# v and z_a of two pairs of heads in one product, with three of eight k-tile pairs as seven products

## The chip, the cores and the metric

The kernel runs on one core of one Trainium2 chip. The metric is the device time of one execution in microseconds. The kernel before takes 1117.3 us (median of 3 runs, 1116.82 to 1117.96). TensorE is PE in the profile, its weight loads PEld, VectorE DVE, ScalarE ACT, GpSimd POOL and SyncE SP.

## The reference

One encoder layer on 256 tokens of width 2048 in f32. Cut to what matters:

```python
hn = rmsnorm(x, norm_w)
q, v, f_fwd, f_bwd, z_a, b_gate, c_gate, h_b, z_b = split(hn @ w_in)      # nine times 2048 columns
o_a = hgrn2(silu(q), v, f_fwd, lb[0]) + hgrn2(silu(q), v, f_bwd, lb[1], reversed)
o_a = head_rmsnorm(o_a, hgrn_norm_w) * silu(z_a)                          # 16 heads of 128
y_b = b_gate * conv3(c_gate * h_b)
o_b = rmsnorm(y_b, conv_norm_w) * silu(z_b)
h = x + concat(o_a, o_b) @ w_out
h = h + (p @ w_ple) * sigmoid(h @ w_ple_gate)
out = rmsnorm(h, final_norm_w)
```

The recurrence runs in chunks of 64 tokens: with the cumulated logarithms of the forget gates f, q and k = 1 - f are scaled, their products are masked (scores), and the scores and the carried states are multiplied with v (outputs).

## The kernel before, in words

*Precision.* Every f32 operand is kept as a high part (rounded to fp32r) and a low part (the rest). One product of 128 rows of k is three matmuls: high x high, high x low, low x high. So every weight passes through `Stream.split` (L98 to L100): ACT casts it to the high part, DVE subtracts. `Stream` loads 1 MB pieces (`raw`, three buffers) on SP's queue, splits them into parts (`spl`, five buffers) and is asked for three parts ahead (`get`).

*Stages.* The layer's 16 heads are eight pairs; `two_pairs(i)` does pairs i and i+1 for i = 0, 2, 4, 6. For each pair it computes f_fwd, f_bwd and q in column-major form, heads on the partitions (`gemm_in`, L378 and L376, 16 k-tiles of four matmuls each), and `evac` (L410, L411) takes the two accumulators out: ACT copies the second half to `r`, DVE adds the first half. Then v and z_a of both pairs, 512 columns each, in token-major form: `gemm_two` (L397 to L399), first v with all 16 k-tiles, then z_a. The accumulators are four banks of PSUM (tag `g`), taken in turn, two by each of these products. After the four groups come the 32 column-major products of branch B, then the output projection `w_out` and the gate `w_ple_gate`.

*Seven products.* The output projection already does four of each eight pairs of k-tiles as seven products of sums instead of eight products (Strassen's scheme, `half`, `three`). The sums of weights are made in DRAM: `prepare` copies the blocks on SP's queue, and `add_up` adds onto them with accumulating DMAs that POOL issues, in three steps, each of which reads what the step before has written. `pump` issues one step; it is called at three places of each pair's attention and once per block of B.

*Attention.* Of a pair: `mix_forgets` (L455) scales f and q by the norms on POOL (`by_norms`, L415), then ACT's sigmoid of f (L459), logarithms `lf` (L469) and the sigmoid of q (L461). `mix_pair` (L513) does scans, exponentials and products, and ends on POOL with `kc`, `qc` (L557) and `kx` (L563). `scores` are 80 small matmuls into banks `sc0`, `sc1` and `x`; `outputs` go to bank `y`; `turn` (L499) transposes a finished pair with PE into `mixa` (L507, L508).

*Order.* The text is recorded with a count of ticks (one per k-tile of `gemm_in`, two per k-tile of v or z_a): `at(n, f)` records f n ticks later, in the middle of the matmuls. A scheduler then sets the order on each engine by priorities: splits and evacuations have high priority, DMAs of `prepare` and `add_up` keep their place in the program's order. Each engine takes its own queue in order.

## Time and profile before

| what | value |
| --- | --- |
| time, median of 3 runs | 1117.3 us (1116.82 to 1117.96) |
| the profiled execution | 1116.78 us, span 1115.1 us |
| PE busy | 1105.2 us (99%) |
| DVE busy | 795.0 us (71%) |
| ACT busy | 660.4 us (59%) |
| POOL busy | 258.8 us (23%) |
| v and z_a of group 2 | 192.3 to 245.1 us of the span, DVE 40.0 us, ACT 35.6 us |
| v and z_a of group 4 | 311.7 to 364.5 us |
| v and z_a of group 6 | 431.1 to 483.9 us |
| DMA | 260.43 MB, mean 234 GB/s |

Times in a timeline are microseconds from the span's start. A row gives start, duration, engine, line, operation and out<-in; a bracket gives the idle time of the engine before it and what ended that. In a row of stretches the engines stand in the order PE, PEld, DVE, ACT, POOL, each with busy time and count, then the granted TensorE clock, the DMA engines' busy share and GB/s. DMA-issuing instructions of POOL have rows of their own.

### The profile page before, as it was taken

Reading aid. Unit: us, or ns where it says so; the run is one execution under the profiler, and the core shown is the slowest. Engines: PE = TensorE matmul, PEld = TensorE weight load, DVE = VectorE, ACT = ScalarE, POOL = GpSimd, SP = SyncE. Lnnn points to the kernel's source line nnn. Section 1 sums busy time; section 2 is a strip of 40 time slices with the busy share of each in tenths; the row PEclk is TensorE's granted clock in tenths of the full one; section 3 lists DMA queues with packets and bytes.
Section 4 is the critical chain, followed back from the end, with each engine's and each line's share of the span. In section 5 each row is a group of like instructions: output and inputs, shape, how many; then the busy total and the mean of one; then the engine's idle time right before and its main releaser. Section 6 shows DMA issues by size and latency. Waiting matters only on the chain.

```text
span 1115.1 us, 16704 instructions
## 1 busy us (share of the span) xinstructions
PE 1105.2 (99%) x6482; PEld 950.5 (85%) x6482; DVE 795.0 (71%) x1040; ACT 660.4 (59%) x920; POOL 258.8 (23%) x215
## 2 busy tenths in 40 slices
PE   9999999999999999999999999999999999999996
PEld 8888888888888888888888888888888888888886
DVE  7898466955967586855666767766657878887663
ACT  7796566756865586664454544544546565575553
POOL 1144026410533036422232231322221000000101
PEclk9999999999999999999999999999999999999999
DMA  9746848765688557859897898887867887887542
GB/s 346 279 171 229 280 171 226 190 208 189 201 261 275 184 173 198 228 184 287 282 230 220 246 279 287 223 225 221 236 184 278 320 295 282 290 311 254 190 132 76
DMA packets 58287, 260.43 MB, mean 234 GB/s; under 512 B 6240, under 2 KB 6624, under 8 KB 40672
## 3 DMA queue, kind: packets, MB, share of 16 engines
q1 hardware_dynamic: 48960, 242.24, 62.7%
q0 software_dynamic: 8960, 16.78, 11.0%
q8 instruction: 51, 0.84, 0.3%
q10 hardware_dynamic: 288, 0.34, 0.1%
q14 instruction: 28, 0.23, 0.1%
HBM read 257.25 MB, written 35.65 MB: 263 GB/s over the span
## 4 chain that ended last, share of the span: by engine, by line
PE 99%; ACT 0%; DVE 0%; DVEq 0%; issue 0%; ACTq 0%
PE a L378 37%; PE a L376 19%; PE a L399 5%; PE a L397 5%; PE a L398 5%; PE pg L844 3%; PE pg L845 3%; PE pg L843 3%; PE pa L850 2%; PE pa L851 2%; PE pa L852 2%; PE pb_sc L852 1%; PE pb_sc L851 1%; PE pb_sc L850 1%; PE scps L577 1%; PE cx L621 1%
## 5 line engine op out<-in xcount | busy, mean ns | idle before, releaser
L100 DVE TENSOR_TENSOR spl<-raw,spl 128x1024 fp32r<-128x1024 f32 (+2 forms) x401 | 491.8, 1237 | 225.4 <-ACT spl L99 223.5
L378 PE MATMUL a<-xs,spl 128*128 128x512 f32 x1792 | 620.0, 394 | 0.0
L99 ACT CAST spl<-raw 128x1024 fp32r<-128x1024 f32 (+2 forms) x401 | 400.6, 1006 | 262.5 <-PE a L376 157.8
L376 PE MATMUL a<-xs,spl 128*128 128x256 f32 x1792 | 493.9, 278 | 0.0
L378 PEld LDWEIGHTS a<-xs,spl 128*128 128x128 f32 x1792 | 335.2, 188 | 76.3
L376 PEld LDWEIGHTS a<-xs,spl 128*128 128x128 f32 x1792 | 336.2, 188 | 2.1 <-DVE spl L100 0.2
L397 PE MATMUL a<-spl,xs 128*128 128x512 f32 x256 | 100.8, 394 | 0.0
L399 PE MATMUL a<-spl,xs 128*128 128x512 f32 x256 | 99.8, 390 | 0.0
L398 PE MATMUL a<-spl,xs 128*128 128x512 f32 x256 | 99.7, 389 | 0.0
L410 ACT COPY r<-a 128x256 f32<-128x256 f32 x112 | 40.8, 367 | 50.3 <-PE a L376 50.3
L1008 POOL TENSOR_TENSOR hh<-hh,fw 128x512 f32<-128x512 f32 (+1 forms) x9 | 11.0, 1226 | 251.4 <-ACT gt L1007 248.8
L399 PEld LDWEIGHTS a<-spl,xs 128*128 128x128 f32 x256 | 48.1, 188 | 10.1
L397 PEld LDWEIGHTS a<-spl,xs 128*128 128x128 f32 x256 | 48.1, 188 | 9.5
L398 PEld LDWEIGHTS a<-spl,xs 128*128 128x128 f32 x256 | 48.1, 188 | 9.5
L415 POOL TENSOR_TENSOR xf<-xf,rbc 128x1024 f32<-128x1024 f32 x8 | 21.1, 2640 | 129.0 <-DVE xf L411 122.1
L843 PE MATMUL pg<-spl,ht 128*128 128x512 f32 (+1 forms) x120 | 45.2, 377 | 0.0
L844 PE MATMUL pg<-spl,ht 128*128 128x512 f32 (+1 forms) x120 | 45.1, 376 | 0.0
L845 PE MATMUL pg<-spl,ht 128*128 128x512 f32 (+1 forms) x120 | 45.1, 376 | 0.0
L557 POOL TENSOR_TENSOR qc<-pf,ge 128x256 f32<-128x256 f32 x16 | 33.8, 2118 | 36.1 <-ACT ge L544 18.2
L99 ACT CAST spl<-early 128x1024 fp32r<-128x1024 f32 (+1 forms) x29 | 28.7, 990 | 19.8 <-PE pb_y L852 7.5
L100 DVE TENSOR_TENSOR spl<-early,spl 128x1024 fp32r<-128x1024 f32 (+1 forms) x29 | 33.0, 1148 | 10.0 <-ACT spl L99 9.5
L850 PE MATMUL pa<-spl,mixa 128*128 128x512 f32 x88 | 34.5, 392 | 0.0
(275 smaller groups left out, 1389.4 us busy)
## 6 DMA issues: line engine op xcount, KB each, us to landing
raw<-in_w_in_dram SPq DMA_DIRECT2D x106, 1024.0 KB, 6.4
raw<-in_w_in_dram SPq DMA_DIRECT2D x74, 512.0 KB, 5.1
raw<-in_w_out_dram SPq DMA_DIRECT2D x36, 512.0 KB, 5.2
sums<-in_w_out_dram SPq DMA_DIRECT2D x32, 512.0 KB, 8.3
raw<-sums SPq DMA_DIRECT2D x13, 1024.0 KB, 6.0
raw<-in_w_gate_dram SPq DMA_DIRECT2D x9, 1024.0 KB, 5.0
sums<-in_w_out_dram POOLq DMA_DIRECT2D x16, 512.0 KB, 8.1
sums<-sums POOLq DMA_DIRECT2D x32, 256.0 KB, 5.6
```

The lines of the kernel that those rows point to most:

```text
L99: self.nc.scalar.copy(out=v[:, :, 0], in_=r)
L100: self.nc.vector.tensor_tensor(out=v[:, :, 1], in0=r, in1=v[:, :, 0], op=ALU.subtract)
L376: pe.matmul(a[:, :T], lhsT=lhsT, rhs=xs[:, kt, 0, :], start=False, stop=(kt == NKT - 1))
L378: pe.matmul(a, lhsT=lhsT, rhs=xs[:, kt, :, :].rearrange("p s n -> p (s n)"), start=(kt == 0), stop=False)
L397: pe.matmul(acc[m], lhsT=lh, rhs=w[:, kt % 2, 0, :], start=(kt == 0), stop=False)
L398: pe.matmul(acc[m], lhsT=lh, rhs=w[:, kt % 2, 1, :], start=False, stop=False)
L399: pe.matmul(acc[m], lhsT=ll, rhs=w[:, kt % 2, 0, :], start=False, stop=(kt == NKT - 1))
L410: act.copy(out=r, in_=acc[m][:, 1, :])
L843: pe.matmul(acc[m], lhsT=lh, rhs=wh, start=(kt == 0), stop=False)
L844: pe.matmul(acc[m], lhsT=lh, rhs=wl, start=False, stop=False)
L845: pe.matmul(acc[m], lhsT=ll, rhs=wh, start=False, stop=(kt == nk - 1))
L850: pe.matmul(acc, lhsT=ah, rhs=w[:, 0], start=start, stop=False)
```

## The change

In groups 2, 4 and 6 `gemm_vz` takes the place of two `gemm_two`: v and z_a are one product with 1024 columns over eight pairs of k-tiles, in four accumulators (all four banks). Pairs 2, 4 and 6 of the k-tiles are seven products, with the extra four accumulators in `x`, `y`, `sc0` and `sc1`. In the first and the last pair v's part of both k-tiles comes ahead of z_a's. Group 0 is as before. The sums of x are made once, in group 2 (`xsums`); the sums of the weights of each group in DRAM, by nine steps at ticks 24 to 96 of the group, with four of w_out's steps set among them. `pump` is no longer called in the attention, but twice per block of B. Since `x`, `y`, `sc0` and `sc1` are in use, of the attention only the first pair's scores stay in v and z_a; the second pair's scores, both outputs and the turns go to the column-major products behind (or, for group 6, to B's first ones). The values are scaled by the norms after the combination.

```diff
-        at(late + 8, lambda: steps[0][0]())
-        at(late + 9, lambda: steps.append(mix_pair(i + 1, *forgets[1])))
-        at(46 if i == 0 else 43, lambda: out(0))
-        at(46 if i == 0 else 43, lambda: steps[1][0]())
-        at(60, lambda: out(1))
-        gemm_two(B_V, i, vt)
...
-        gemm_two(B_ZA, i, zt)
+        else:
+            at(4, lambda: steps[0][0]())
+            gemm_vz(i, vt, zt)
+            at(8, lambda: steps.append(mix_pair(i + 1, *forgets[1])))
+            at(12, lambda: out(0))
+            at(28, lambda: steps[1][0]())
+            at(40, lambda: out(1))
...
-                    at((56, 108)[e], lambda e=e: turn(i + e, ogs[e], "yx"[e]))
+                    at(36 + 6 * e, lambda e=e: turn(i + e, ogs[e], "yx"[e]))
```
```diff
+        if i:
+            todo = vz_prepared[i]
+            for z, what in enumerate(todo):
+                at(8 * z, lambda what=what: prepare(what))
+            turns = [lambda what=what, step=step: add_up(what, step) for step in range(3) for what in todo]
+            for j in (3, 7, 11, 12):
+                turns.insert(j, pump)
+            for j, fn in enumerate(turns):
+                at(24 + 6 * j, fn)
```
```diff
+    def gemm_vz(i, vt, zt):
+        acc = [psg.tile([P, 512], F32, tag="g", name=f"avz{i}_{b}") for b in range(4)]
+        sc = [t.rearrange("p a b -> p (a b)") for t in scps]
+        def extra():
+            x, y = (psm.tile([P, 512], F32, tag=t, name=f"e{t}{i}") for t in "xy")
+            return [x, y, *sc]
+        main = [[acc[m], acc[2 + m]] for m in range(2)]
+        for q1, q5, q6, q7 in half(main, extra, range(8), VZ_SUMS, blocks[B_V, i], xs, xq[0], True):
+            d = xq[1][:, 0]
+            with tc.high_priority(offset=400):
+                act.copy(out=vt[:, 0], in_=q1)
+                dve.tensor_tensor(out=d, in0=vt[:, 0], in1=q6, op=ALU.subtract)
+                dve.tensor_tensor(out=zt[:, 0], in0=q5, in1=d, op=ALU.subtract)
+                dve.tensor_tensor(out=vt[:, 1], in0=d, in1=q7, op=ALU.subtract)
+                dve.tensor_tensor(out=zt[:, 1], in0=zt[:, 0], in1=q7, op=ALU.add)
...
+            for n, dst in enumerate((vt, zt)):
+                for m in range(2):
+                    dve.tensor_tensor(out=dst[:, m], in0=main[m][n], in1=dst[:, m], op=ALU.add)
```

Three places show what the scheduler makes of it, in group 2 (groups 4 and 6 are alike). First POOL's queue before v and z_a: `kx2` ends the first pair's preparation, `xf3` and `qt3` are the second pair's forget gates and q, `sums0_0` are w_out's sums. Before:

```order
L557 TENSOR_TENSOR kc2_1647<-dd2_1625,ge2_1634 128x256
L563 TENSOR_TENSOR kx2_1653<-kc2_1647,ge2_1634 128x512
L291 DMA sums0_0_3_82<-in_w_out_dram 256x1x512
L415 TENSOR_TENSOR xf3_1656<-xf3_1656,rbc_175 128x1024
L415 TENSOR_TENSOR qt3_1657<-qt3_1657,rbc_175 128x512
```

With the change (`vz2_2`, `vz2_4` and `vz2_6` are the sums of group 2):

```order
L695 TENSOR_TENSOR kx2_1707<-kc2_1701,ge2_1688 128x512
L318 DMA vz2_4_82<-vz2_4_82 128x512
L318 DMA vz2_6_83<-vz2_6_83 128x512
L314 DMA sums0_0_3_91<-in_w_out_dram 256x1x512
L318 DMA vz2_2_81<-vz2_2_81 128x512
L318 DMA vz2_4_82<-vz2_4_82 128x512
L318 DMA vz2_6_83<-vz2_6_83 128x512
L314 DMA sums0_0_4_92<-in_w_out_dram 256x1x512
L314 DMA sums0_0_5_93<-in_w_out_dram 256x1x512
L470 TENSOR_TENSOR xf3_1709<-xf3_1709,rbc_184 128x1024
L470 TENSOR_TENSOR qt3_1710<-qt3_1710,rbc_184 128x512
```

One DMA issue between `kx` and `xf` has become eight; the second issue on `vz2_4` reads what the first one on it writes, and so for `vz2_6`. Second, ACT's queue at the start of v and z_a. Before, with `a0_3` q's accumulators of pair 3 and `spl64` the first part of v:

```order
L99 CAST spl65_1887<-raw32_1865 128x2x512
L459 ACT_TABLE_LOAD
L459 ACTIVATE xf3_1656<-xf3_1656 128x1024
L99 CAST spl66_1909<-raw33_1906 128x2x512
L469 ACT_TABLE_LOAD
L469 ACTIVATE lf3_1941<-xf3_1656,lb_171,oml_172 128x256
L99 CAST spl67_1952<-raw33_1906 128x2x512
L469 ACTIVATE lf3_1941<-xf3_1656,lb_171,oml_172 128x256 x2
L410 COPY r_1928<-a0_3_0_1844 128x256
L99 CAST spl68_1970<-raw34_1967 128x2x512
```

With the change:

```order
L101 CAST spl66_1991<-raw33_1986 128x1024
L639 ACTIVATE mixa_499<-ogt1_1968,vec_108 128x256
L592 ACT_TABLE_LOAD
L592 ACTIVATE xf3_1709<-xf3_1709 128x1024
L101 CAST spl67_2036<-raw33_1986 128x1024
L639 ACTIVATE mixa_499<-ogt1_1968,vec_108 128x256
L101 CAST spl68_2050<-raw34_2045 128x2x512
L465 COPY r_2011<-a0_3_0_1902 128x256
L465 COPY r_2014<-a0_3_1_1903 128x256
L601 ACT_TABLE_LOAD
L601 ACTIVATE lf3_2023<-xf3_1709,lb_180,oml_181 128x256 x3
```

The sigmoid of `xf3` has moved back by one cast and now has two casts, and no `lf`, between it and the copies of q's accumulators; in groups 4 and 6 a table load and one `lf` stand ahead of the second of these casts. Third, PE at the start of v and z_a, from the end of the first pair's scores (`scps`): `avz2_2` and `avz2_3` are z_a's accumulators, in the banks of `a0_3`; v's are `avz2_0` and `avz2_1`.

```order
L708 MATMUL scps1_174<-pf2_1678,dd2_1679 32x64
L708 MATMUL scps1_174<-pf2_1678,dd2_1679 32x32 x3
L752 MATMUL cx2_2099<-qc2_1702,kx2_1707 128x128 x4
L525 MATMUL avz2_2_2034<-spl64_1938,xs_183 128x512
L526 MATMUL avz2_2_2034<-spl64_1938,xs_183 128x512
L527 MATMUL avz2_2_2034<-spl64_1938,xs_183 128x512
L525 MATMUL avz2_3_2035<-spl64_1938,xs_183 128x512
```

Ahead of these rows stand the twelve matmuls of v's first two k-tiles and the rest of the first pair's scores. Before, z_a's accumulators came into use with the 97th matmul of the stage; now z_a follows v's first two k-tiles and the scores, as the 13th.

More of the change, by code (lines that the diff above doesn't have):

```diff
@@ L147, in tile_hymba_encoder @@
     ws = Stream(tc, rawp, splp, 3)
+    VZ_SUMS = (2, 4, 6)
+    dramp = ctx.enter_context(tc.tile_pool(name="dramp", bufs=1, space=bass.MemoryType.DRAM))
+    vz_prepared = {}
     blocks = {}
@@ L153, in tile_hymba_encoder @@
                 blocks[c, ii] = sum((ws.add(w_in[c + ii, h]) for h in range(2)), [])
+        if i:
+            blocks[B_V, i], vz_prepared[i] = [], []
+            for q in range(8):
+                srcs = [
+                    [w_in[c + i + b, q // 4, :, 2 * (q % 4) : 2 * (q % 4) + 2] for b in range(2)] for c in (B_V, B_ZA)
+                ]
+                if q in VZ_SUMS:
+                    sums = dramp.tile([P, 4, 512], F32, name=f"vz{i}_{q}")
+                    vz_prepared[i].append((srcs, sums))
+                    blocks[B_V, i].append(ws.add_sums(*srcs, sums))
+                else:
+                    blocks[B_V, i].append(ws.add(*srcs[0], *srcs[1]))
+            continue
         for c in (B_V, B_ZA):
@@ L171, in tile_hymba_encoder @@
                 k = 16 * half + 2 * q
-                srcs = [w_out[2 * u + n, k // 4, :, k % 4 : k % 4 + 2] for n in range(2)]
+                srcs = [[w_out[2 * u + n, k // 4, :, k % 4 : k % 4 + 2]] for n in range(2)]
                 if q in SUMS:
@@ L449, in tile_hymba_encoder, with act_sums, act_split @@
     at(14, norms_spread)
+    def act_sums(src, a, s):
+        dve.tensor_tensor(out=a, in0=src[:, :, 0], in1=src[:, :, 1], op=ALU.add)
+        a11, a21, a12, a22 = (a[:, k, m * P : (m + 1) * P] for k in range(2) for m in range(2))
+        for o, x, y in ((0, a21, a22), (1, a21, a11), (2, a11, s[:, 0]), (3, a12, s[:, 2])):
+            dve.tensor_tensor(out=s[:, o], in0=x, in1=y, op=ALU.subtract)
+    def act_split(dst, src, s):
+        n = dst.shape[1]
+        for d, r in ((dst, s[:, 0:n]), (src[:, 0:1, :, P:], s[:, n:])):
+            if r.shape[1]:
+                act.copy(out=d[:, :, 0], in_=r)
+                dve.tensor_tensor(out=d[:, :, 1], in0=r, in1=d[:, :, 0], op=ALU.subtract)
@@ L949, in tile_hymba_encoder @@
                     act_split(sumb[:, z], mixb[:, k : k + 2], sumb32[z])
-            for q1, q5, q6, q7 in half([acc[0:2], acc[2:4]], lambda: four(other, "e" + name), parts, src, sums):
+            extra = lambda: four(other, "e" + name)
+            for q1, q5, q6, q7 in half([acc[0:2], acc[2:4]], extra, ORDER, SUMS, parts, src, sums, False):
                 d, v, d7, v7 = tmps
```

182 lines of the change are left out of this document (109 added, 73 removed).

## The prediction

> **What bounds the kernel now.** I read the page first: its span, the engines' busy time and the chain that ended last.
>
> ```profile
> span 1115.1 us, 16704 instructions
> PE 1105.2 (99%) x6482; PEld 950.5 (85%) x6482; DVE 795.0 (71%) x1040; ACT 660.4 (59%) x920; POOL 258.8 (23%) x215
> PE 99%; ACT 0%; DVE 0%; DVEq 0%; issue 0%; ACTq 0%
> ```
>
> PE is the chain from end to end, so a matmul less is worth its own pitch, and whatever makes PE wait is paid in full. Next come the three stages that change, v and z_a of the groups i = 2, 4 and 6, as stretches, and two rows of PE's timeline there.
>
> ```profile
> 192.30:245.10 52.80, 52.80 (x410) 44.78 (x409) 40.01 (x49) 35.60 (x59) 15.92 (x16) 1.00 0.74 204
> 311.70:364.50 52.80, 52.80 (x410) 44.79 (x409) 39.62 (x49) 35.25 (x59) 15.29 (x15) 1.00 0.87 253
> 197.79:200.50 2.71, 2.71 (x93) 2.50 (x92) 2.71 (x5) 2.71 (x7) 0.00 (x0) 1.00 0.26 62
> ```
> ```profile
> 192.31 0.39 PE L397 MATMUL a<-spl,xs 128*128 128x512 f32 x1
> 192.54 0.39 PE L398 MATMUL a<-spl,xs 128*128 128x512 f32 x1
> ...
> 197.79 0.60 PE L504 MATMUL ogt<-ident,ogz 128*128 128x128 f32 x4
> 198.32 0.30 PE L577 MATMUL scps<-qc,dd 128*32 128x128 f32 x2
> ...
> 311.72 0.39 PE L397 MATMUL a<-spl,xs 128*128 128x512 f32 x1
> ...
> 431.12 0.39 PE L397 MATMUL a<-spl,xs 128*128 128x512 f32 x1
> ```
>
> PE has no gap, and a 512-column matmul starts every 0.23 us (the 0.39 is latency). Turning one pair's output takes 0.5 us (197.79 to 198.32); the next pair's scores take the other 2.2 us of the short stretch. DVE is at 40.0 of 52.8 us here, so it has some room and not much.
>
> Then I asked what ACT and POOL do ahead of such a stage, because all the weights of TensorE pass through ACT and DVE. POOL's timeline in groups 2, 4 and 6, then ACT's:
>
> ```profile
> 187.96 1.05 POOL L563 TENSOR_TENSOR kx<-kc,ge 128x512 f32<-128x512 f32 x1
> 188.95 1.06 POOL L291 DMA_DIRECT2D sums<-in_w_out_dram  x1
> 189.55 2.90 POOL L415 TENSOR_TENSOR xf<-xf,rbc 128x1024 f32<-128x1024 f32 x1
> ...
> 308.14 0.83 POOL L291 DMA_DIRECT2D sums<-sums  x1
> 308.70 2.69 POOL L415 TENSOR_TENSOR xf<-xf,rbc 128x1024 f32<-128x1024 f32 x1
> ...
> 427.62 1.06 POOL L291 DMA_DIRECT2D sums<-in_w_out_dram  x1
> 428.22 2.89 POOL L415 TENSOR_TENSOR xf<-xf,rbc 128x1024 f32<-128x1024 f32 x1
> ```
> ```profile
> 185.27 1.28 ACT L459 ACT_TABLE_LOAD   x1
> 192.49 1.06 ACT L459 ACTIVATE xf<-xf 128x1024 f32<-128x1024 f32 x1 [5.94 <-POOL xf L415]
> 193.45 1.03 ACT L99 CAST spl<-raw 128x1024 fp32r<-128x1024 f32 x1
> ...
> 195.80 0.60 ACT L469 ACTIVATE lf<-xf,lb,oml 128x256 f32<-128x256 f32 x1
> ...
> 198.24 0.35 ACT L410 COPY r<-a 128x256 f32<-128x256 f32 x1
> ...
> 204.10 0.46 ACT L507 ACTIVATE mixa<-ogt,vec 128x256 fp32r<-128x256 f32 x1
> ...
> 311.42 1.06 ACT L459 ACTIVATE xf<-xf 128x1024 f32<-128x1024 f32 x1 [5.46 <-POOL xf L415]
> ...
> 431.14 1.06 ACT L459 ACTIVATE xf<-xf 128x1024 f32<-128x1024 f32 x1 [5.79 <-POOL xf L415]
> ```
>
> This is the row to keep: at the start of each such stage ACT already stands 5.5 to 5.9 us in front of the sigmoid of the odd pair's forget gates, because POOL scales them last. The weight casts queue behind it. PE rides it out on parts split beforehand, and the evacuation of q's accumulators, behind the same sigmoid (198.24), is awaited by nobody until z_a's product 26 us later.
>
> **The change, part by part.** *Matmuls.* A k-tile pair costs 24 matmuls plain and 21 as seven products; three pairs in three groups save 27. 27 x 0.228 = **-6.2 us**. Scores, outputs and turns are moved, not removed: 0.
>
> *Extra work off PE.* Each seven-product pair brings 1536 more elements to split (about 1.5 splits), each group eight 512-wide combinations, and x's sums once. These lie under PE while DVE has room; without that cover they are the DVE rival below. The evacuations at the stage's end are ordered so that v's banks are written 12 matmuls, 2.7 us, before the end, and v's two additions hide under z_a's: 0. A 512-wide one takes 0.69:
>
> ```profile
> L927 DVE TENSOR_TENSOR hh<-pa,hh 128x512 f32<-128x512 f32 x8 | 5.1, 687 | 0.0
> ```
>
> *The sums in DRAM, and POOL's queue.* Each group now has nine vz steps (twelve issues, the first step of each tensor being two) and four of w_out's on POOL. By the order shown with the change, eight stand in a row between `kx` and the scaling of the next pair's `xf`, where one stood. The fifth (vz_4's last step) reads what the first writes, so POOL, which takes its queue in order, waits for a landing; behind it are `xf`, then `qt`, ACT's sigmoid, the casts behind that, and everything that feeds on them. The prices, from the issues and landings of before:
>
> ```profile
> L291 POOL DMA_DIRECT2D sums<-sums x32: 791/819/947, 224.0 to 832.1; - x32
> DMA to landing us min/median/max: 4.4/7.0/10.6
> ```
>
> From issue to the next POOL operation the timeline shows 0.56 to 0.60 us. A landing takes 7.0 at the median; I take that (batches of 512 KB share the queue). `xf` then starts at the first issue + 7.0 + 4 x 0.6 = 9.4 us instead of 0.6: **8.8 us later**. Bounds: with no landing wait at all, 7 issues x 0.6 = 4.2; with the longest, 12.4.
>
> The Trainium skill, page "DMA: Bandwidth & Descriptors", section "Anatomy of one DMA — SWDGE (gpsimd) path", says that DMA engines do not wait on semaphores; a wait is served on the issuing sequencer before dispatch. No run here shows POOL in such a wait; by that rule POOL stands still as I assume, and were it otherwise the delay would be the 4.2 of the lower bound.
>
> *Where that delay lands.* The accumulators are four banks in turn. Before, v took two that had long been free. Now v and z_a take all four, and z_a's two are q's, evacuated only after the delayed sigmoid. z_a's first matmul would be due 12 matmuls (2.73) plus the scores (2.2) = 4.9 us into the stage. The stage itself starts 1.0 us later relative to POOL, since two turns (2 x 0.5) now come ahead of it. Group 2, in us after its start: the sigmoid at 192.49 - 193.31 + 8.8 = 8.0; then on ACT, each from its start to the next one's, sigmoid 1.0, cast 1.0, a `mixa` 0.4, cast 1.0 (11.4); then DVE, in rows of the same stage:
>
> ```profile
> 198.84 0.41 DVE L411 TENSOR_TENSOR qt<-a,r 128x256 f32<-128x256 f32 x1
> ...
> 199.56 1.23 DVE L100 TENSOR_TENSOR spl<-raw,spl 128x1024 fp32r<-128x1024 f32 x1
> ```
>
> the split 1.2 and q's addition 0.4: 13.0, so PE waits 8.1 us. In groups 4 and 6 a table load (1.3) and one `lf` (0.5) stand ahead of that cast too; their sigmoids come at 311.42 - 312.72 + 8.8 = 7.5 and at 431.14 - 432.12 + 8.8 = 7.8, z_a at 14.3 and 14.6: waits of 9.4 and 9.7. Together **+27.2 us**; with the bounds, 4.6 less each (13.4) or 3.6 more each (38.0). What follows z_a is late as well, but ACT and DVE have the same 8 to 10 us to catch up, so I add nothing.
>
> *TensorE's clock.* A wait this long has a price of its own. After the last matmul the granted clock is full for 5 us, then halved:
>
> ```profile
> 1106.40:1111.40 5.00, 0.00 (x0) 0.00 (x0) 3.28 (x10) 2.79 (x5) 0.72 (x1) 1.00 0.75 279
> 1111.50:1115.10 3.60, 0.00 (x0) 0.00 (x0) 0.00 (x0) 0.00 (x0) 0.00 (x0) 0.50 0.40 153
> ...
> 1.13 5.27 PE L224 MATMUL wps<-wz 128*128 128x128 f32 x26 [1.13 <-DVE wz L219]
> ...
> 6.21 0.47 PE L378 MATMUL a<-xs,spl 128*128 128x512 f32 x1
> ```
>
> At the start the dummy matmuls run about 4.5 us before the pitch is that of later. Waits of 8 to 10 us are over 5, so I take a fall each, and some 4.4 us at half speed after it: 2.2 lost, **+6.6 us** (bounds 0 and 6.6).
> The Trainium skill, "TensorE: Matmul & The Clock Gate", section "Part 1: The HAM clock gate (the "warmup" mystery)", puts both windows at about 3.4 us; by it the loss would be 1.7 a wait, 5.1 in all, and even the waits of the lower bound would meet it. The trace here shows 5 us to the fall, which decides for the sum.
>
> Sum: 1116.8 (the profiled execution: span 1115.1 and 1.7 around it; the median of the runs is 1117.3, 0.5 above) - 6.2 + 27.2 + 6.6 = 1144.4. The clock term stands at its upper bound, so I take a little off and say **1143 us**. The mechanism's own range is 1116.8 - 6.2 + 13.4 = 1124 to 1116.8 - 6.2 + 38.0 + 6.6 = 1155.
>
> **Rivals.**
> (a) *The gain stays.* POOL's batch gets out earlier, or PE meets no delayed evacuation: 1117.3 - 6.2 = 1111. For it: PE rode out 5.9 us of ACT's wait without a gap. Against: that cover was two banks which now have to be empty at 4.9 us. It turns from faster to slower where the three waits pass 2.1 us each, that is where `xf` comes about 2 us later than now.
> (b) *DVE becomes the bound.* Work of a stage: 40.0 + 3 x 1.5 splits x 1.23 (5.5) + 8 x 0.7 (5.6) less what moved out (a turn's four, one pair's two mask copies, two output copies of 0.7, together 4.8) = 46.3 us against 183 x 0.228 + 2.2 = 43.9: 2.4 late, three times 7.2: 1118, no change. Against: part of it may stand ahead of the stage.
>
> ```profile
> L508 DVE SCALAR_TENSOR_TENSOR mixa<-ogt,vec,mixa 128x256 fp32r<-128x256 f32 x16 | 7.6, 479 | 2.3 <-ACT mixa L507 2.3
> L625 DVE COPY_PREDICATED early<-early,scps 128x512 f32<-128x512 uint32 x16 | 11.7, 739 | 1.7 <-PE scps L577 1.7
> ```
>
> (c) *Transfers become the bound.* By the page's queue shares, loads move 346 GB/s at full use and POOL's sums 137:
>
> ```profile
> q1 hardware_dynamic: 48960, 242.24, 62.7%
> q0 software_dynamic: 8960, 16.78, 11.0%
> ```
>
> A stage now loads 8.4 + 2.4 MB (31 us), and the batch, 2.1 to 2.9 MB, takes 15 to 21: 46 to 52 us of 44, 13 in all if nothing is loaded ahead: 1117.3 - 6.2 + 13 = 1124. Inside the forecast's waits it would be hidden, as ACT would be the later one.
>
> **How the numbers follow.** The forecast (POOL's batch holds ACT, z_a waits) has 0.76, (c) alone 0.06, (b) 0.06, (a) 0.12. A measurement of this kernel tells 0.2% (2.2 us) from no change. Faster takes (a) and a little of (b): 0.13; the same, most of (b): 0.05; slower the rest: 0.82. The range runs from 1122 (below the lower bound of the mechanism, taking in (c)) to 1157; it leaves out (a) and (b), 0.18.
>
> **What would show it.** On POOL, eight DMA issues in a row after `kx` with a pause before the fifth, and `xf` scaled some 8 us into the stage; on ACT, the idle time ahead of the `xf` sigmoid 13 to 15 us instead of 5.9; on PE, one gap of 8 to 10 us in each of three stages ahead of the first matmul into z_a's accumulator, released by the evacuation of `qt`, and a granted clock under 1.00 there; 27 fewer 512-wide matmuls. I am wrong if PE has no gap there (then POOL got its issues out in time), if the gaps stand at splits released by a load, or if DVE is busy without a pause through the stage.

## The result, and the profile after

The changed kernel takes 1164.9 us (median of 4 runs, 1161.15 to 1171.35) where the kernel before takes 1117.1 on the same chip: a ratio of 1.043, interval 1.039 to 1.048. That is slower, as forecast, but by 47.8 us instead of 26, and outside the range. The page of the changed kernel first: span, engines, and the chain that ended last.

```profile
span 1162.7 us, 17008 instructions
PE 1111.8 (96%) x6455; PEld 951.6 (82%) x6455; DVE 825.8 (71%) x1100; ACT 681.5 (59%) x948; POOL 300.4 (26%) x251
PE 70%; DVE 8%; POOL 7%; ACT 7%; DMA 5%; issue 3%; SPq 0%; DVEq 0%; ACTq 0%; POOLq 0%
```

PE was the whole chain before; now 30% of it lies on others. The 27 matmuls are gone (6482 to 6455). The three stages of v and z_a, as stretches (PE, PEld, DVE, ACT, POOL, granted clock, DMA share, GB/s):

```profile
195.20:253.70 58.50, 47.72 (x273) 37.93 (x272) 39.07 (x51) 34.82 (x44) 22.68 (x15) 0.91 0.86 250
327.70:386.90 59.20, 47.02 (x273) 38.58 (x272) 40.55 (x52) 33.98 (x44) 16.72 (x16) 0.88 0.79 233
460.90:525.00 64.10, 47.38 (x274) 38.48 (x272) 40.56 (x52) 34.03 (x44) 18.45 (x19) 0.87 0.75 214
```

With 183 matmuls of 0.228 us and one pair's scores (2.2) such a stage should take 43.9 us. The three lose 14.6, 15.3 and 20.2: 50.1 us. Where, PE's timeline says:

```profile
208.25 2.05 PE L752 MATMUL cx<-qc,kx 128*128 128x128 f32 x8 [8.86 <-DVE mixa L640]
209.95 0.78 PE L525 MATMUL avz<-spl,xs 128*128 128x512 f32 x1
...
344.01 2.05 PE L752 MATMUL cx<-qc,kx 128*128 128x128 f32 x8 [12.10 <-DVE mixa L640]
...
480.65 2.05 PE L752 MATMUL cx<-qc,kx 128*128 128x128 f32 x8 [15.53 <-DVE mixa L640]
```

One wait in each stage, 36.5 us in all, not before z_a's first matmul but just ahead of it, in the scores: their last part goes to bank `x`, which the second turn still holds until `mixa` is copied out. Behind it is the chain of the forecast. POOL in group 2:

```profile
189.68 1.05 POOL L695 TENSOR_TENSOR kx<-kc,ge 128x512 f32<-128x512 f32 x1
190.67 1.67 POOL L318 DMA_DIRECT2D vz<-vz  x2
191.74 1.68 POOL L314 DMA_DIRECT2D sums<-in_w_out_dram  x1
192.30 1.95 POOL L318 DMA_DIRECT2D vz<-vz  x1
196.31 0.80 POOL L318 DMA_DIRECT2D vz<-vz  x1 [2.05 <-DMA vz<-vz]
199.12 0.81 POOL L318 DMA_DIRECT2D vz<-vz  x1 [2.02 <-DMA vz<-vz]
199.65 2.41 POOL L314 DMA_DIRECT2D sums<-in_w_out_dram  x2
200.79 3.64 POOL L470 TENSOR_TENSOR xf<-xf,rbc 128x1024 f32<-128x1024 f32 x1
```

The eight issues stand there, the fifth and the sixth wait for landings, and `xf` starts 10.1 us after the first issue (9.4 forecast; 9.4 and 11.1 in groups 4 and 6). ACT and DVE behind it, and ACT's sigmoid in groups 4 and 6:

```profile
204.46 1.06 ACT L592 ACTIVATE xf<-xf 128x1024 f32<-128x1024 f32 x1 [11.50 <-POOL xf L470]
...
206.36 0.47 ACT L639 ACTIVATE mixa<-ogt,vec 128x256 fp32r<-128x256 f32 x1
...
207.66 0.64 ACT L465 COPY r<-a 128x256 f32<-128x256 f32 x2
...
336.34 1.06 ACT L592 ACTIVATE xf<-xf 128x1024 f32<-128x1024 f32 x1 [10.98 <-POOL xf L470]
...
472.98 1.06 ACT L592 ACTIVATE xf<-xf 128x1024 f32<-128x1024 f32 x1 [12.82 <-POOL xf L470]
```
```profile
207.63 0.48 DVE L640 SCALAR_TENSOR_TENSOR mixa<-ogt,vec,mixa 128x256 fp32r<-128x256 f32 x1
...
209.15 0.75 DVE L466 TENSOR_TENSOR qt<-a,r 128x256 f32<-128x256 f32 x2
```

Both copies that free banks stand behind the sigmoid; `qt`, for z_a's bank, ends at 209.9, and z_a's first matmul stands at 209.95: number 4 below shows that z_a waits for them by itself. Last the clock, in group 4's wait and after it:

```profile
337.00:344.00 7.00, 0.00 (x0) 0.02 (x1) 4.45 (x8) 6.95 (x13) 0.45 (x1) 0.50 1.01 318
346.30:350.20 3.90, 3.90 (x11) 3.04 (x10) 3.90 (x4) 1.00 (x2) 3.43 (x3) 0.51 0.01 4
```

Work after the wait runs at half speed for 5.3 to 6.2 us; by the pitch of the matmuls that costs about 8.4 us in the three stages. The last 5.2 of the 50.1 are small waits, among them 1.35 us each at the end of groups 2 and 6, where the next product's bank is still being added out. Outside the stages group 0 ends 2.0 us later. Of this 1.4 lie in its v and z_a, where the scheduler has moved x's sums (53.3 us instead of 51.9); the rest lies in its column products, which take 67.7 to 69.7 us in the versions below.

### The profile page after: what moved, and what is told of

Its sections match the earlier page's. It is cut to its first block, busy times and chain, and to the rows that moved or that the text cites. A ratio compares the mean times of both kernels' runs of the same rounds, so it can differ in the third digit from the quotient of the medians.

```text
span 1162.7 us, 17008 instructions
## 1 busy us (share of the span) xinstructions
PE 1111.8 (96%) x6455; PEld 951.6 (82%) x6455; DVE 825.8 (71%) x1100; ACT 681.5 (59%) x948; POOL 300.4 (26%) x251
## 3 DMA queue, kind: packets, MB, share of 16 engines
q0 software_dynamic: 16448, 26.22, 15.3%
## 4 chain that ended last, share of the span: by engine, by line
PE 70%; DVE 8%; POOL 7%; ACT 7%; DMA 5%; issue 3%; SPq 0%; DVEq 0%; ACTq 0%; POOLq 0%
PE a L405 26%; PE a L403 13%; DVE spl L102 4%; DMA raw<-in_w_in_dram 3%; PE pg L995 3%; PE pg L994 3%; PE pg L993 3%; ACT spl L101 2%; DMA vz<-vz 2%; PE pa L525 2%; PE pa L527 2%; PE pa L526 2%; POOL kc L689 2%; PE avz L526 1%; PE avz L525 1%
## 5 line engine op out<-in xcount | busy, mean ns | idle before, releaser
L102 DVE TENSOR_TENSOR spl<-raw,spl 128x1024 fp32r<-128x1024 f32 (+2 forms) x419 | 500.1, 1209 | 238.7 <-ACT spl L101 236.6
L101 ACT CAST spl<-raw 128x1024 fp32r<-128x1024 f32 (+2 forms) x419 | 412.5, 998 | 268.2 <-PE a L403 120.5
L526 PE MATMUL avz<-spl,xs 128*128 128x512 f32 x138 | 56.6, 410 | 0.7 <-DVE spl L102 0.7
L525 PE MATMUL avz<-spl,xs 128*128 128x512 f32 x138 | 56.8, 411 | 0.0
L527 PE MATMUL avz<-spl,xs 128*128 128x512 f32 x138 | 55.7, 404 | 0.0
L752 PE MATMUL cx<-qc,kx 128*128 128x128 f32 x64 | 11.9, 344 | 37.5 <-DVE mixa L640 36.5
L470 POOL TENSOR_TENSOR xf<-xf,rbc 128x1024 f32<-128x1024 f32 x8 | 28.1, 3518 | 66.9 <-DVE rbc L381 49.1
L752 PEld LDWEIGHTS cx<-qc,kx 128*128 128x128 f32 x64 | 10.2, 242 | 38.1 <-issue 36.7
L689 POOL TENSOR_TENSOR kc<-dd,ge 128x256 f32<-128x256 f32 x16 | 33.2, 2072 | 29.0 <-DVE dd L680 16.5
L592 ACT ACTIVATE xf<-xf 128x1024 f32<-128x1024 f32 x8 | 8.5, 1060 | 45.1 <-POOL xf L470 45.0
```

The costliest lines, as they stand in the source:

```text
L101: self.nc.scalar.copy(out=v[:, :, 0], in_=r)
L102: self.nc.vector.tensor_tensor(out=v[:, :, 1], in0=r, in1=v[:, :, 0], op=ALU.subtract)
L525: pe.matmul(acc, lhsT=ah, rhs=w[:, 0], start=start, stop=False)
L526: pe.matmul(acc, lhsT=ah, rhs=w[:, 1], start=False, stop=False)
L527: pe.matmul(acc, lhsT=al, rhs=w[:, 0], start=False, stop=stop)
L689: pool.tensor_tensor(out=c64(dst[:, d]), in0=c64(src[:, d, :, half * P : (half + 1) * P]), in1=g.unsqueeze(3).broadcast_to([P, 2, 2, CH]), ...
```

## The experiments

Ticks are the counter of `at`; a diff is against the changed kernel unless it says otherwise. Each ratio is to the kernel before, run on the same chip.

**1. The odd pairs' forget gates scaled on DVE.**

```diff
-        by_norms(xf.rearrange("p a b t -> p (a b) t"), rbc, 4)
+        by_norms(xf.rearrange("p a b t -> p (a b) t"), rbc, 4, dve if i % 2 else pool)
```

> The changed kernel with one edit: the odd pairs' forget gates are scaled by the norms on DVE, right behind their evacuation, instead of on POOL behind the eight DMA issues. All DMAs, sums and seven products stay. Theory (POOL's batch holds ACT's sigmoid, and through it the evacuations that free the banks PE needs): the three PE gaps of 9.0, 12.3 and 15.7 us at the start of v and z_a fall under 2 us each, the granted clock stays 1.00, and 1164.9 - 37 - 7 of clock = about 1121 us (1115 to 1128). Rival, DVE is the bound of these stages: DVE gets 3 x 1.1 us more, so no gain, 1162 or more. Rival, the transfers are the bound: the gaps stay, 1155 to 1165.

Measured: 1152.8 us, ratio 1.033 (1.029 to 1.038). The gaps at the scores are gone (0, 0.3 and 1.5 us), and only 12 of the 44 us came back. PE, ACT and SP's queue in group 2 of this run:

```profile
216.31 0.80 PE L525 MATMUL ey<-spl,xsum 128*128 128x512 f32 x1 [5.35 <-ACT spl L101]
```
```profile
215.22 1.04 ACT L101 CAST spl<-raw 128x1024 fp32r<-128x1024 f32 x1 [6.88 <-DMA raw<-vz]
```
```profile
186.45 1.88 SPq L76 DMA_DIRECT2D raw<-in_w_in_dram  x4
206.51 0.33 SPq L76 DMA_DIRECT2D raw<-vz  x1
```

A second wait lay under the first. SP's queue stood from 188 to 206.5 before it could issue the load of the sums, since POOL's last step on them had not landed (its wait of 18 us ends with a landing of `vz<-vz`); PE reaches the first pair of seven products and waits 5.4 us there. None of the three expectations had this.

**2. No landing waited for in the batch; 3. no accumulating DMAs on vz; 4. the turns 12 ticks earlier.**

```diff
-            dst, src = ((3, 0), (1, 3))[step - 1]
+            dst, src = ((3, 0), (1, 2 if n_of(what) else 3))[step - 1]   # 2: vz sums only
...
-                at(24 + 6 * j, fn)
+                at(24 + 6 * j, fn if fn is pump else lambda: None)           # 3
...
-                at(30, lambda: finish_two(ogs, ss, zt, ogs))
+                at(18, lambda: finish_two(ogs, ss, zt, ogs))                 # 4
...
-                    at(36 + 6 * e, lambda e=e: turn(i + e, ogs[e], "yx"[e]))
+                    at(24 + 6 * e, lambda e=e: turn(i + e, ogs[e], "yx"[e]))
```

> The changed kernel, but the third step of each vz sum reads a row that the first step has finished instead of the row that the second step writes: as many DMAs of the same size, and none of the batch waits for a landing of the batch (the sums, and so the output, are other ones). Theory: POOL's batch shrinks by its two waits, 2.05+2.02, 1.80+1.82 and 4.93+0.46 us in the three groups; xf, sigmoid and PE's gaps shrink by as much, 13.1 us: about 1152 us (1148 to 1157). Rival, the issues or the transfers themselves cost it, not the waits for landings: within 3 us of 1164.9.

> The changed kernel without the accumulating DMAs of the vz sums (the blocks are still copied and loaded; the sums, and so the output, are other ones); w_out's steps stay where they are. Theory: three issues instead of eight ahead of xf, so xf comes 8.4, 7.7 and 9.4 us earlier in the three groups; of PE's gaps 0.6, 4.6 and 6.3 us are left, with at most one fall of the clock: about 1135 us (1122 to 1140). Rival, the banks that four accumulators and the turns share make PE wait whatever POOL does: over 1150.

> The changed kernel with the turns of the pairs before 12 ticks earlier (8 us), so that the copies out of bank x stand ahead of the sigmoid on ACT and the scores' last four matmuls find the bank free. Theory as forecast (z_a waits for the evacuation of q's accumulators in any case): the gap moves from the scores' last matmuls to z_a's first, released by DVE's addition into qt, and the time stays within 5 us of 1164.9. Rival, bank x alone is what PE waits for: the gaps go, 1130 or less.

Measured: 1154.9 (1.030 to 1.036), 1147.1 (1.023 to 1.029) and 1157.2 us (1.033 to 1.037). The landings waited for cost 10 us, inside the theory's range; the gaps shrink to 4.9, 8.6 and 10.5. Without the steps the time lies between the theory's range and the rival's: gaps of 4.3, 5.4 and 4.8 us stay. POOL in the run without landing waits shows an issue's price:

```profile
191.55 1.67 POOL L321 DMA_DIRECT2D vz<-vz  x2
...
195.89 5.44 POOL L473 TENSOR_TENSOR xf<-xf,rbc 128x1024 f32<-128x1024 f32 x1
```

Eight issues in a row start 0.55 us apart, and then `xf` takes 5.44 us. In the run with three issues it takes 3.88, before the change, with one, 2.9. From first issue to the end of `xf` are 9.8 us with eight, 5.6 with three: some 0.85 to 1.1 us an issue, with 2.4 for `xf` itself, as an `xf` without an issue ahead of it shows (number 5). The forecast had 0.6.

With the turns early, PE in group 2:

```profile
209.52 0.77 PE L525 MATMUL avz<-spl,xs 128*128 128x512 f32 x1 [8.23 <-DVE qt L466]
```

The wait is the forecast's one, for `qt`, as expected. The time fell by 7.7 instead of staying: in groups 4 and 6 the gaps are 4.2 and 5.9 instead of 12.1 and 15.5, while the turns now wait for their operands (2.6 and 3.3 us) and the column products with them take 78.3 and 79.8 us instead of 74.0, so that the stages start later. Bank `x` alone is refuted, and the two banks bind one behind the other.

**5 and 6. The same DMAs earlier: the blocks copied one stage ahead, all steps in the first 40 ticks; 6 also with `xf` on DVE.**

```diff
-            for j, fn in enumerate(turns):
-                at(24 + 6 * j, fn)
+            for j, fn in zip((0, 1, 2, 6, 7, 7, 20, 22, 24, 28, 32, 36, 40), turns + [pump] * 4):
+                at(j, fn)
...
+        for z, what in enumerate(vz_prepared.get(i + 2, ())):
+            at(4 + 6 * z, lambda what=what: prepare(what))
```

> The changed kernel with the same DMAs issued earlier: the blocks of the vz sums are copied one stage ahead, and all nine vz steps and the four steps of w_out stand on POOL in the first 40 ticks of a group, ahead of the scaling of the even pair; between kx and the odd pair's xf stands no issue. Theory (when POOL issues its batch is what costs the time, on ACT's way and, as the run with xf on DVE showed, on SP's queue, which stood at a load of sums that were not ready): no issue ahead of xf makes it 3 us earlier than without the vz steps, so 1.2, 2.3 and 1.8 us of PE's gaps stay, no load of vz holds SP in the stage, 1117.3 - 6.2 + 5.3 + about 7 of the other losses seen (x's sums in group 0, the evacuation at a stage's end) = 1123 us (1115 to 1130). Rival, the seven products cost DVE or the transfers as much as they save, wherever the steps stand: 1135 or more.

> As the run before, and the odd pairs' forget gates scaled on DVE. Theory: the sigmoid no longer hangs on POOL at all, the gaps of 1 to 2 us at the scores go too: 1117 us (1110 to 1123), the better of the two. Rival: DVE has no room, so equal to the run before or slower.

Measured: 1156.4 (1.033 to 1.036) and 1146.4 us (1.024 to 1.027): far above the theory. No issue stands ahead of `xf`, and PE still waits 3.6, 2.9 and 3.7 us at the scores in the first of the two. In groups 2 and 4, where the next group's blocks are copied in the stage, seven products wait for loads and splits as well (stages of 60.7 and 58.9 us); group 6, which copies none, takes 51.9, and with `xf` on DVE 47.1. That the copies make the difference is argued from this; no run took them out by themselves.

**7. No seven products: the joined product, its four banks and the moved attention alone. 8. The same, with the odd pairs' sigmoid held at its place in the text.**

```diff
-    VZ_SUMS = (2, 4, 6)
+    VZ_SUMS = ()
...
-            for j in (3, 7, 11, 12):
-                turns.insert(j, pump)
+            for j in (28, 32, 36, 40):
+                at(j, pump)
...
-        act.activation(xf, xf, AF.Sigmoid)
+        sig = act.activation(xf, xf, AF.Sigmoid)       # 8 only
+        if i % 2 and i > 1:
+            tc.keep_in_program_order(sig)
```

> The changed kernel with no seven products in v and z_a (all eight pairs of k-tiles plain, no vz sums, no sums of x used), the four steps of w_out in ticks 28 to 40: the joined product, its four banks and the attention among the column products alone. Theory: with no DMA issue ahead of xf the banks cost 1 to 2 us a stage and the evacuations at its end 1.4: 1117 + 5 + 4 = 1126 us (1120 to 1130). Rival, the four banks and the attention's new place hold PE up by themselves: 1140 or more. Rival, they cost nothing: 1117.

> The run without seven products (1131 us; PE's gaps at the scores 3.8, 3.0 and 3.0 us though no DMA issue stood ahead of xf), and the odd pairs' sigmoid keeps its place in the text on ACT: behind the copies that free bank x and q's accumulators, which stood behind it. Theory (what is left there is ACT's order: the copies behind sigmoid, table load and logarithms): the gaps go, 1131 - 12 = 1119 us (1117 to 1122). Rival, the joined product costs in another way (its evacuations, the attention's new place): 1127 or more.

Measured: 1131.1 (ratio 1.011, 1.009 to 1.013), 1.1 us above the theory's range, and 1118.3 us (1.0001, 0.9991 to 1.0012), as the theory had it. PE and ACT in the first:

```profile
203.35 1.36 PE L752 MATMUL cx<-qc,kx 128*128 128x128 f32 x8 [3.62 <-DVE mixa L640]
...
327.43 2.04 PE L752 MATMUL cx<-qc,kx 128*128 128x128 f32 x8 [2.86 <-DVE mixa L640]
...
451.30 1.13 PE L752 MATMUL cx<-qc,kx 128*128 128x128 f32 x8 [2.86 <-DVE mixa L640]
```
```profile
193.44 1.06 ACT L592 ACTIVATE xf<-xf 128x1024 f32<-128x1024 f32 x1 [4.24 <-POOL xf L470]
...
201.39 0.48 ACT L639 ACTIVATE mixa<-ogt,vec 128x256 fp32r<-128x256 f32 x1
```

The sigmoid comes 2 us before the stage starts, no DMA issue stands ahead of POOL's `xf`, and still the last `mixa` leaves ACT 8 us later: ACT first waits 4.2 us for the plain `xf` and is then busy with the table load, logarithms and casts that the scheduler set ahead of the copy. With the sigmoid held back until the copies are done, every stage of the second run is full (the first is shown):

```profile
195.20:241.10 45.90, 45.90 (x282) 38.10 (x281) 32.46 (x41) 28.54 (x35) 11.04 (x9) 1.00 0.54 184
```

So the joined product and the new place of the attention cost nothing by themselves: what costs is the order on ACT, with the copies behind a sigmoid that waits for POOL, 12.8 us even without a single DMA too many.

**9. The changed kernel with that one line; 10 and 11. also with its DMAs early in their own group (11 with x's sums held in group 2); 12. number 9 without the accumulating DMAs on vz.** The line is that of number 8; 10 calls `prepare` at ticks 0, 4 and 8, the vz steps at 20 to 44 and w_out's at 26, 36, 46 and 47.

> The changed kernel with that one edit: all DMAs stay where they are, POOL's batch still holds the sigmoid as long, but the copies stand ahead of it. Theory: no gap at the scores; the loads of the vz sums, which SP issues late since the steps are late, bind next, as in the run with xf on DVE: 1150 us (1143 to 1155). Rival, the sigmoid's wait holds the casts behind it and PE waits for those just as long: 1160 or more. Rival, only the copies mattered: under 1130.

> As the run before, and the DMAs early within their own group: the blocks copied at ticks 0 to 8, the nine vz steps at ticks 20 to 44, w_out's among them, all ahead of the even pair's scaling on POOL and none in a v and z_a stage. Theory: neither the copies nor a load of late sums holds PE; 1117.3 - 6.2 + 3 x 2.5 (the evacuation at a stage's end, 1.4, and a split waited for, 1) + 1.9 (x's sums in group 0) + 1.2 = 1122 us (1115 to 1128). Rival, the seven products' own work (DVE, transfers) costs more than they save by much: 1135 or more.

> As the run before, with x's sums kept at their place in group 2 instead of in group 0 (and a higher priority for the evacuation of v and z_a). Theory: group 0 is again as long as before the change, 1.9 us less than the run before, 1120 us (1113 to 1126); if it is also under the kernel before, seven products pay once nothing waits for them. Rival, x's sums hid all along: no difference.

> The run with only the sigmoid kept behind the copies (1153.5 us), without the accumulating DMAs of the vz sums (the blocks are copied and loaded; the sums, and so the output, are other ones). It leaves of the change's costs only the seven products' own work on ACT, DVE and in the loads. Theory (the late landing of the sums is what still holds SP's queue, and PE at the first seven product by 3.5, 1.2 and 5.2 us): those gaps go; what stays is the evacuation at a stage's end (1.4) and a split or two in its middle (2 to 4), 1117.3 - 6.2 + 3 x 5 + 3 = 1129 us (1122 to 1137). Rival, the work of the seven products is itself too much for ACT and DVE: 1145 or more.

Measured: 1153.5 (1.030 to 1.034), 1179.7 (1.052 to 1.060), 1175.2 (1.049 to 1.057) and 1137.8 us (1.016 to 1.020). Number 9 has the theory's number, but not its wait: at the first pair of seven products PE waits for an evacuation in all three groups (3.4, 1.0 and 5.0 us), and not for a load. That the number came out is luck.

```profile
212.78 0.50 PE L525 MATMUL ex<-spl,xs 128*128 128x512 f32 x1 [3.36 <-ACT sx L761]
216.64 0.51 PE L526 MATMUL ey<-spl,xsum 128*128 128x512 f32 x1 [1.26 <-DVE spl L102]
...
341.65 0.50 PE L525 MATMUL ex<-spl,xs 128*128 128x512 f32 x1 [1.04 <-ACT sx L761]
...
473.31 0.80 PE L525 MATMUL ex<-spl,xs 128*128 128x512 f32 x1 [5.02 <-ACT sx L761]
```

The copy `sx` out of bank `x` stands behind the sigmoid too, so POOL's batch reaches PE a third way. Numbers 10 and 11 are the worst of all. POOL in group 6 of number 10, and PE:

```profile
439.62 0.81 POOL L318 DMA_DIRECT2D vz<-vz  x1 [7.81 <-DMA vz<-vz]
...
448.04 3.26 POOL L470 TENSOR_TENSOR xf<-xf,rbc 128x1024 f32<-128x1024 f32 x1
```
```profile
455.54 0.79 PE L405 MATMUL a<-xs,spl 128*128 128x512 f32 x1 [12.18 <-ACT spl L101]
```

The landings are now waited for ahead of the even pair's `xf`, ACT's casts stand behind its sigmoid, and PE waits 12 us in the middle of a column product. Moving the steps moved the wait. Holding x's sums brings group 0's v and z_a back to 51.9 us (53.2 in number 10); the rest of the 4.5 us between the two numbers is inside the scatter.

Number 12 is 0.8 us above its range: without the steps, and with ACT in order, the stages still take 49.9 to 53.3 us. Its first and third stage, a part of the first, and DVE there:

```profile
195.90:245.80 49.90, 47.08 (x273) 38.23 (x272) 40.06 (x51) 32.24 (x41) 11.42 (x10) 0.93 0.80 241
445.30:498.60 53.30, 46.93 (x274) 37.03 (x272) 40.26 (x53) 33.27 (x43) 11.89 (x12) 0.97 0.72 227
205.00:212.00 7.00, 7.00 (x32) 5.79 (x32) 7.00 (x16) 5.15 (x8) 0.00 (x0) 1.00 0.60 198
212.00:220.00 8.00, 5.18 (x17) 3.70 (x16) 8.00 (x9) 5.94 (x9) 6.43 (x5) 0.77 0.35 131
```
```profile
213.01 1.72 DVE L682 TENSOR_TENSOR dd<-xf,dd 128x512 f32<-128x512 f32 x2
214.65 1.10 DVE L683 TENSOR_TENSOR pf<-qt,pf 128x512 f32<-128x512 f32 x1
215.68 5.79 DVE L102 TENSOR_TENSOR spl<-raw,spl 128x1024 fp32r<-128x1024 f32 x4
```

DVE is busy for 40 of 50 us in a stage, 33 with plain products, but from 205 to 220 without a pause: the odd pair's preparation falls between the splits of the first seven products, and PE waits 2.6 us for one of them (2.3 in its row).

**13 and 14. Late pairs.** Pairs 4, 5 and 6 instead of 2, 4 and 6, the sigmoid and x's sums held, the third steps issued behind the odd pair's `qt`; in 14 the first two steps ahead of the even pair.

```diff
-    VZ_SUMS = (2, 4, 6)
+    VZ_SUMS = (4, 5, 6)
...
+            for j, fn in zip((24, 30, 36, 54, 60, 66, 97, 97, 98), turns):   # 14: 4, 6, 7, 26, 30, 34, 97, 97, 98
+                at(j, fn)
```

> The changed kernel with the sigmoid kept behind the copies, x's sums kept in group 2, the pairs 4, 5 and 6 instead of 2, 4 and 6 as seven products, and the third step of the vz sums issued after the odd pair's xf and qt. As many matmuls as the changed kernel; the sums are needed 22 us after a stage's start instead of 11. Theory: steps that land late cost nothing where the pair comes late; 1117.3 - 6.2 + 3 x 3.5 + 1 = 1122 us (1112 to 1132). Rival, the landings are too late even so (steps behind qt's product on POOL, 5 us into the stage, then two landings of 8): PE waits some 5 us at pair 4 in each stage, 1138 or more.

> As the run before, with the first two steps of the vz sums ahead of the even pair on POOL (first steps in ticks 4 to 7, second steps in ticks 26 to 34) and w_out's steps in ticks 40, 44, 102 and 106. Theory: the landings are waited for where POOL has idle time (22 us ahead of the mask's copies in groups 4 and 6), so nothing is late and the stage stands as in the run before, 1119 us (1110 to 1128). Rival, the even pair's scaling comes late again, as in the run with all steps early: 1140 or more.

Measured: 1139.8 (1.017 to 1.020) and 1156.3 us (1.033 to 1.036). Both are the rival's numbers. Number 13 is the best of the versions that keep seven products and their sums (number 16 is inside its scatter), 25 us under the changed kernel and 22 above the one before; its gaps are 0.5 to 2.3 us each, most at the first products of a sum. Number 14 waits again in the column products: those of groups 4 and 6 take 81.6 and 90.0 us instead of 73.7.

**15 to 18. What holds the middle of a stage.** 15 is number 12, and 16 number 13, with four products of the odd pair's preparation on POOL; 17 and 18 are the same two with weights split four parts ahead.

```diff
-            dve.tensor_tensor(out=dv[d], in0=xf[:, d], in1=dv[d], op=ALU.mult)
-            dve.tensor_tensor(out=pv[d], in0=qt, in1=pv[d], op=ALU.mult)
+            eng = pool if i % 2 and i > 1 else dve                            # 15, 16
+            eng.tensor_tensor(out=dv[d], in0=xf[:, d], in1=dv[d], op=ALU.mult)
+            eng.tensor_tensor(out=pv[d], in0=qt, in1=pv[d], op=ALU.mult)
...
-    ws = Stream(tc, rawp, splp, 3)
+    ws = Stream(tc, rawp, splp, 4)                                            # 17, 18
```

> The run with the sigmoid kept and without the accumulating DMAs of the vz sums (1137.8 us; the sums, and so the output, are other ones), where DVE was busy without a pause for 15 us in the middle of a stage while PE waited 2.6 us for a split. Now four 512-wide products of the odd pair's preparation (3.9 us of DVE a stage, between these splits) are done by POOL. Theory, DVE is what the seven products' own work runs into: the gap of 2.6 us and half of the smaller ones go, with the slow clock behind them: 1137.8 - 3 x 4 = 1126 us (1121 to 1131). Rival, the loads or ACT's casts hold the splits: within 4 us of 1137.8. Rival, POOL's products take DVE's time as well: no gain or slower.

> The run with the late pairs 4, 5 and 6 (1139.8 us, output as the reference), with the same four products on POOL. Theory: DVE binds there too, around pair 4: 1139.8 - 3 x 3 = 1131 us (1124 to 1136). Rival: its gaps stand at the first products of sums that land late, and POOL has more to do ahead of the next steps: 1138 or more.

> The run with the sigmoid kept and without the accumulating DMAs of the vz sums (1137.8 us; its output is another one), with weights split four parts ahead instead of three (the five buffers allow no more). In a plain pair a part is 12 matmuls, so three parts ahead cover 36 matmuls, 8.2 us; of seven products the four parts are 6, 3, 6 and 6 matmuls, so three cover 15 to 18, 3.4 to 4.1 us, while the odd pair's exponentials stand 5 us ahead of casts on ACT in both. Theory (the look-ahead is counted in parts and shrinks where a part carries half the matmuls): one more part is 1.4 us more cover, the gaps in the middle of a stage (0.8, 0.8 and 2.6 us) shrink by about that and the slow clock behind them ends in part: 1137.8 - 3 x 2.5 = 1130 us (1125 to 1134). Rival, the work itself is too much for ACT and DVE, whatever the look-ahead: within 3 us of 1137.8.

> The run with the late pairs 4, 5 and 6 (1139.8 us, output as the reference), also with four parts ahead. Theory: as in the run before, 1139.8 - 3 x 2.5 = 1132 us (1126 to 1137). Rival: its gaps are landings of sums, and no part split ahead helps: 1138 or more.

Measured: 1136.1 (ratio 1.019, 1.015 to 1.022), 1141.0 (1.020 to 1.023), 1144.9 (1.022 to 1.027) and 1144.2 us (1.021 to 1.025). None is a gain clear of the scatter. Numbers 15, 16 and 18 lie where their rivals have them; 17 is 7 us slower than number 12, which neither theory nor rival had (in group 6 z_a waits 4.1 us for `qt` again). DVE in the middle of number 15:

```profile
215.46 9.71 DVE L102 TENSOR_TENSOR spl<-raw,spl 128x1024 fp32r<-128x1024 f32 x6 [1.74 <-ACT spl L101]
```

DVE is free there now and waits for a cast, which stands on ACT behind the same preparation's exponentials; and its splits take 1.62 us each beside POOL's products, 1.45 in number 12, 1.23 where POOL rests. So neither four products less on DVE nor one part more of look-ahead gives the time back. That DVE plays no part is not shown, since POOL's products held its splits up (last section).

The 20 us between numbers 12 and 8 are not the seven products' alone: number 12 also has three of w_out's issues ahead of the odd pair's `xf`. In group 2 this does not show at the sigmoid, which comes 2.8 us into the stage in both, and the stage is still 4.0 us longer with nine matmuls less. In groups 4 and 6 the sigmoid is 2.5 us later in number 12, behind a split that stands 5.4 us beside POOL. How much of the 20 us that is, and how much an order of ACT's and DVE's queues made for seven products would give back, is left open.

## Why the prediction was wrong

**The sum, term by term.** The matmuls: 27 went. The step that failed is the size of the waits, put at 8.1, 9.4 and 9.7 us, 27.2 in all, and measured at 8.9, 12.1 and 15.5, 36.5 in all. The chain from POOL's batch over the sigmoid to the banks is there, step by step, but its last link is another: the wait begins 0.7 us earlier in each stage, at the scores' last matmuls, which I had counted as work ahead of the wait, and it is for bank `x`, which the second turn holds and which the forecast did not have; `qt` comes right behind. The wait's end is where the forecast had it in group 2, 13.0 us into the stage, and 2.0 and 5.1 us later in groups 4 and 6. In group 2 that is luck: the sigmoid is 1.2 us late, and the way from it to the release 1.2 us shorter. In the other two the sigmoid is 1.1 and 4.2 us late and the way 0.9 longer.

**The sigmoid.** It comes at 9.2, 8.6 and 12.0 us of the stage instead of 8.0, 7.5 and 7.8. The landing of the first steps ends 5.6, 5.1 and 8.3 us after the first issue instead of 7.0; the sixth issue waits for one more (2.0, 1.8 and 0.5 us), which the sum did not have. An issue costs POOL 0.85 to 1.1 us and not 0.6: I took the spacing of the rows and passed over the 0.82 that a row itself takes; the rest hides in the next operation's length. In group 6 the batch itself begins 2.4 us ahead of the stage instead of the 4.5 that 3.5 before and the turns' 1.0 would give, probably since the first steps stand ahead of the even pair's `xf` as well; no run shows this by itself. I had moved the stage against POOL by the turns and not POOL against the stage.

**The clock.** 6.6 forecast, about 8.4 measured. The fall comes 4.0, 4.5 and 4.5 us after the last matmul, near the 5 of the trace before, but half speed lasts 5.3, 6.2 and 5.9 us and not 4.4.

**"I add nothing."** Two places that were costed at nothing cost something: the small waits behind the stall and the evacuation at a stage's end, 5.2 us, and group 0, 2.0 us, of which x's sums are 1.4. With 9.3 of the waits and 1.8 of the clock that is 18.3 of the 20.0 us by which the profiled execution (1164.4) stands above the sum (1144.4).

**The rivals** were the larger mistake. I gave (b) and (c) 0.06 each, as ways instead of the forecast's, and wrote of (c) that inside the waits it would be hidden. What was hidden was there. Taking the causes off one after the other gives 1164.9, 1153.5 with ACT's copies ahead of the sigmoid, 1137.8 also without the accumulating DMAs on vz, 1118.3 also without seven products (and with w_out's steps ahead of the even pair). So the wait that I forecast at 27 and that PE shows at 36.5 is worth 11 to 12 us when it alone is taken off (numbers 9 and 1), and the seven products, which were to gain 6.2 us, lose up to 19.5 even when their sums cost no accumulation. Part (b) had the right place and the wrong reason: DVE is busy for 40 us of a stage, not the 46 that I counted, and it is its order, with ACT's, that delays a split. Of (c) there was a load that SP issued late (number 1), not the queue shares from which I had reckoned.

**What was not seen.** Number 7 shows that the batch of issues is not needed for a wait: ACT's order, with the sigmoid 2 to 3 us ahead of the stage and its old wait for POOL's `xf` (3.5 to 4.2 us), makes the scores wait 2.9 to 3.6 us. I read the order of ACT's rows correctly and took from it only where the sigmoid stood, not that ACT had no pause behind it.

## What to carry to other kernels

A long wait hides the next ones: 36.5 us of waits and the slow clock behind them gave back 12 here, so look at what would be late next (the load of the same sums, the next split) before adding up. Where nothing stood behind, in numbers 7 and 8, waits of 9.3 us were worth 12.8. When accumulators are made to take all banks, whatever frees a bank must stand ahead, in its engine's own queue, of any operation that can wait for another engine; one instruction held at its place was worth 12.8 us here. A chain of DMAs that feed each other holds its issuing engine at a landing wherever two links stand close: POOL waited 13 us for landings of `vz<-vz` in the changed kernel, 34 in number 10, where the chain was moved earlier and held up what was queued there, and 3 in number 13, with the last link far behind.

## What the runs showed of the hardware

An issue of a DMA on POOL takes 0.85 to 1.1 us of POOL's own time, although the next row starts 0.55 us later: the operation behind carries the rest in its length, 2.4 us alone, 2.9 behind one issue, 3.9 behind three, 5.4 behind eight. The Trainium skill, "Perfetto Trace Analysis", section "DMA Instruction — SWDGE (GPSIMD)", says that GpSimd's own processors write the descriptors and that such a row ends when the last of them has written its last one, not when the data have moved. The trace agrees on the end: rows of 0.8 to 1.05 us, landings 4.4 to 10.6 us after the issue in the kernel before. What fills a row no run here shows.

The clock fell after shorter waits than the 5 us that the end of the trace before suggested. In number 7 two waits of 2.86 us stand in the same place of two groups: behind one the eight matmuls of `cx` take 2.04 us and the next ones run at half speed, behind the other they take 1.13. In the first the granted clock fell 2.4 us after the last matmul, in the changed kernel 4.0 to 4.5 us after it. The Trainium skill, "TensorE: Matmul & The Clock Gate", section "Part 1: The HAM clock gate (the "warmup" mystery)", has free-running windows of about 3.4 us. The falls seen here lie on both sides of that figure.

DVE's splits of 128x1024 took 1.23 us, but 1.45 and 1.62 on the mean where POOL multiplied at the same time. The rows show how: a split that meets POOL's `xf` ends 1.09 us after `xf` does, however long that is. Two cases of number 12:

```profile
193.05 3.87 POOL L470 TENSOR_TENSOR xf<-xf,rbc 128x1024 f32<-128x1024 f32 x1
194.37 3.64 DVE L102 TENSOR_TENSOR spl<-raw,spl 128x1024 fp32r<-128x1024 f32 x1 [0.48 <-ACT spl L101]
...
314.68 5.44 DVE L102 TENSOR_TENSOR spl<-raw,spl 128x1024 fp32r<-128x1024 f32 x1 [0.58 <-ACT spl L101]
315.74 3.29 POOL L470 TENSOR_TENSOR xf<-xf,rbc 128x1024 f32<-128x1024 f32 x1
```

`xf` ends at 196.92 and 319.03, the splits at 198.01 and 320.12. In number 8 it is the same with an `xf` of 2.40 us (311.85 and 312.94), and most of the long splits of the other runs end like this. So such a split stands until POOL is done and then takes its time, and its length counts as busy. No run was made for this alone.
